# Attention heads on one Trainium2 core: each round's operations put in the order in which their inputs arrive

## The chip, the cores and the metric

One core of one Trainium2 chip runs the whole program in one launch. The metric is device time in microseconds (us). Engines: TensorE (PE in the rows, with PEld for its weight loads), VectorE (DVE), ScalarE (ACT), GpSimd (POOL) and SyncE (SP), which issues the DMA transfers.

## The reference, cut to what matters

Two layers over 512 frames of 1024 channels, float32. The first has a gated linear attention, the second chunked softmax attention with 16 heads of 64 channels; each is followed by a squared-ReLU MLP, and each sub-layer ends in a LayerNorm. The change sits in the softmax attention of the second layer:

```
q, k, v = jnp.split(u @ w_in + b_in, 3, axis=-1)
...
s = jnp.einsum('bhtd,bhjd->bhtj', qi, kb).astype(jnp.float32) + bias
p = jax.nn.softmax(jnp.where(mb, s, NEG_INF), axis=-1).astype(vb.dtype)
return jnp.einsum('bhtj,bhjd->bhtd', p, vb)
...
return o @ w_out
...
x = layer_norm(DEEPNORM_ALPHA * x + (1.0 + g1) * y, ln_g[i, 0], ln_b[i, 0])
```

## The kernel before

Activations lie with channels on partitions and the 512 frames along the row. A matrix product in float32 is made of three passes over a high and a low part of each operand, so for each weight tile and each activation ScalarE casts a high part and VectorE subtracts to get the low one.

Every engine runs its instructions strictly in the order in which the program text emits them: the wrapper `InOrder` (line 47 in every row is its line) chains each engine's instructions. So the text's order is each engine's queue, and an instruction that waits holds up all behind it on its engine. SyncE's DMA issues stand in text order too.

The attention (`att`) works on pairs of heads. `for p in range(-1, 6)` is the round: it makes q and k of head pair p+2 (`mtile`, 24 matmuls each, then `evac_qk`), works on the scores of heads 2p+2 (even) and 2p+3 (odd), and multiplies pair p with v. After the loop, heads 14 and 15 and the end of 12 and 13 are done in the functions `t1` to `t5`, which the list `ev` mixes with the output projection (`part`, called in `boundary`). The steps and how they look in the rows:

- `s_mm(h)`: TensorE, 8 matmuls, scores of one head (`ps<-ar,ar`).
- `s_a(h)`: VectorE adds the bias window (`af<-ps,ng,af`, 4 instructions) and takes maxima (3), with ScalarE copies; then GpSimd reduces the maximum over partitions (`mb<-af`, PARTITION_ALL_REDUCE).
- `s_b1(h)`: VectorE subtracts that maximum (`af<-af,mb`, 4). `s_b2(h)`: ScalarE's exponential (`af<-af` 128x1024 and 128x256). `s_b(h)` is both.
- `pv(h)`: TensorE, 4 matmuls with v (`ps<-af,vt`), which also give the softmax denominator.
- `fin1(p)`: the division's ScalarE part for a pair: two copies from PSUM (`af<-ps` 64x512), logarithm and exponential (`af<-af` 128x512). `fin2(p)`: its VectorE part (4 instructions: `af<-af` twice, `af<-ps,af` twice). `fin3(p)`: bias and split into high (ScalarE, `ar<-af,col`) and low (VectorE, `ar<-af,col,ar`).
- `q_hi`, `k_hi`: ScalarE casts of a new q or k (`ar<-f`), behind its evacuation (`f<-ps,bq` or `f<-ps,col`); `q_lo`, `k_lo`: VectorE's two subtractions (`ar<-f,ar` 64x512). The next pair's s_mm needs them.
- `s_pre(h)`: the DMA of a head's bias window (`af<-a_win`). `fill(n)`: weight transfers ahead of use.
- `ln_cols`: five VectorE operations on 8 columns that prepare a LayerNorm's scale and shift (`a`, `b`, `b`, `ag`, `ab`).

Before, fin1, fin2 and s_b1(odd) open a round, in this order, and s_b2(odd) comes after s_a(even); s_b2(even) closes it. The last round (p = 5) has an order of its own, in which s_b1(12) and s_b2(12) are left to `t1`. ln_cols for the following LayerNorm is called at the start of `boundary`, after the attention's loop is emitted.

Of the kernel before, what the change touches and what calls it, by code (L numbers as in the profile page):

```python
# [59 lines left out]
def trunk(ctx, tc, xT, c, ada, cols, gk1, gk2, w_qk, w_v, w_g, w_go, a_qk, a_v, a_tab,  # L60
# [239 lines left out]
    def mtile(u, f=True):  # L300
        w = next_w(f)
        ps = bank()
        for k in range(KT):
            mm3(ps, wk(w, k), uk(u, k), k == 0, k == KT - 1)
        return ps
# [665 lines left out]
    def att(u, es):  # L971
# [11 lines left out]
        def s_pre(h):  # L983
            sA, sB = act_f(), act_f()
            b = sB[:, 0, 256:S]
            nc.sync.dma_start(out=b, in_=a_win[h])
            sab[h] = sA, sB, b
# [4 lines left out]
        def s_mm(h):  # L992
            p = h // 2
            q, k = qs[p], ks[p]
            pss = [bank()[:, 0:S], bank()[:, 0:384]]
            pl = bank()
            pss += [pl[:, 0:256], pl[:, 256:S]]
            for j in range(4):
                ps = pss[j]
                n = max(W[j], 256)  # L1000
                js = slice(j * P, (j + 1) * P)
                T.matmul(ps[:, 0:n], k[:, h % 2, js], q[:, h % 2, S - n:S], start=True, stop=False)
                T.matmul(ps[:, 0:n], k[:, h % 2, js], ql[p][:, h % 2, S - n:S], start=False, stop=True)
            sps[h] = pss
# [26 lines left out]
        def s_b1(h):  # L1031
            s, sAf = st[h]
            mb = mbs[h]
            tt(V, s[0], s[0], mb, ALU.subtract)
            tt(V, s[1], s[1], mb[:, P:S], ALU.subtract)
            tt(V, s[2], s[2], mb[:, 256:S], ALU.subtract)
            tt(V, s[3], s[3], mb[:, 384:S], ALU.subtract)
# [15 lines left out]
        o = []  # L1053
# [3 lines left out]
        def fin1(p, pa, pb):  # L1057
            sy = act_f()
            s, y = sy[:, 0, :], sy[:, 1, :]
            A.copy(out=s[0:64, :], in_=pa[64:128, :])  # L1060
            A.copy(out=s[64:128, :], in_=pb[0:64, :])
            A.activation(out=y, in_=s, func=AF.Ln)
            A.activation(out=y, in_=y, func=AF.Exp, scale=-1.0)
            fin[p] = s, y, pa, pb

        def fin2(p):
            s, y, pa, pb = fin[p]
            tt(V, s, s, y, ALU.mult)
            stt(y, s, 2.0, y, ALU.subtract, ALU.mult)
            stt(s[0:64, :], pa[0:64, :], -1.0, y[0:64, :], ALU.mult, ALU.mult)  # L1070
            stt(s[64:128, :], pb[64:128, :], -1.0, y[64:128, :], ALU.mult, ALU.mult)
# [17 lines left out]
            fill(2)  # L1089
        prev = None  # L1090
        for p in range(-1, 6):
            pq = mtile(u, False)
            s_pre(2 * p + 2)
            s_pre(2 * p + 3)
            if prev:
                fin1(*prev)
                fin2(p - 1)
            if p >= 0:
                s_b1(2 * p + 1)
            s_mm(2 * p + 2)  # L1100
            q_hi, q_lo = evac_qk(p + 2, 0, pq)
            if p == 5:
                q_hi()
                q_lo()
                fill(2)
            if prev:
                fin3(p - 1)
            if p < 5:
                s_a(2 * p + 2)
                if p >= 0:  # L1110
                    s_b2(2 * p + 1)
                fill(2)
                q_hi()
                q_lo()
                pk = mtile(u, False)
                s_mm(2 * p + 3)
                k_hi, k_lo = evac_qk(p + 2, 1, pk)
                s_a(2 * p + 3)
                k_hi()
                s_b1(2 * p + 2)  # L1120
                k_lo()
                fill(2)
                s_b2(2 * p + 2)
            else:
                pk = mtile(u, False)
                k_hi, k_lo = evac_qk(p + 2, 1, pk)
                s_b2(2 * p + 1)
                k_hi()
                s_a(2 * p + 2)
                k_lo()  # L1130
                s_mm(2 * p + 3)
                s_a(2 * p + 3)
                fill(2)
            if p >= 0:
                prev = (p, pv(2 * p), pv(2 * p + 1))
        s_pre(14)
# [8 lines left out]

        def t1():
            s_mm(14)
            s_b1(12)
            s_a(14)
            s_b2(12)  # L1150
            fill(2)
            s_b(13)

        def t2():
            s_mm(15)
            s_a(15)
            fill(2)
            fin1(*prev)
            s_b(14)
            fin2(5)  # L1160

        def t3():
            s_b1(15)
            fin1(6, hold[12], hold[13])
            fin3(5)
            s_b2(15)
            fin2(6)
            fill(3)
# [65 lines left out]
    hs = run(u, 0)  # L1234
    u = boundary(hs, 0, G2, open_v, lambda: ln_cols(0, 1, (1, SH1, SC1)), None, vfill=vfill)
    cur["es"].close()
    o, ev, es = att(u, cur["es_v"])
    evac_h, run = mlp_fns()
    u = boundary(o, 1, G1, opener(es, 1), lambda: ln_cols(1, 0, (1, SH2, SC2)), evac_h, ev, late=True)
    hs = run(u, 1)  # L1240
    boundary(hs, 1, G2, same, lambda: ln_cols(1, 1, None), None, final=True)
    cur["es"].close()
# [52 lines left out]
```

## Time and profile before

| | |
|---|---|
| runs, median of 3 | 1212.07 us (1211.79 to 1212.17) |
| profiled execution | 1211.67 us, its span 1209.8 us |
| busy share of the span | TensorE 97%, VectorE 68%, ScalarE 46%, GpSimd 4% |
| granted TensorE clock, mean | 0.994 of full speed (2.4 GHz) |

The span is the time from the first to the last instruction that the profile holds; the rest of the execution lies around it. Times in the rows below are counted from the span's start. The attention's loop lies at about 637 to 767 us, its tail at 767 to 805. A row of a timeline gives start, duration, engine, line, operation, output and inputs, and the number of instructions merged in it; in brackets stands the idle time of the engine ahead of it and who ended it.

### The profile page before, as it was taken

Reading aid. Unit: us, or ns where it says so; the run is one execution under the profiler, and the core shown is the slowest. Engines: PE = TensorE matmul, PEld = TensorE weight load, DVE = VectorE, ACT = ScalarE, POOL = GpSimd, SP = SyncE. Lnnn points to the kernel's source line nnn. Section 1 sums busy time; section 2 is a strip of 40 time slices with the busy share of each in tenths; the row PEclk is TensorE's granted clock in tenths of the full one; section 3 lists DMA queues with packets and bytes.
Section 4 is the critical chain, followed back from the end, with each engine's and each line's share of the span. In section 5 each row is a group of like instructions: output and inputs, shape, how many; then the busy total and the mean of one; then the engine's idle time right before and its main releaser. Section 6 shows DMA issues by size and latency. Waiting matters only on the chain.

```text
span 1209.8 us, 15107 instructions
## 1 busy us (share of the span) xinstructions
PE 1177.0 (97%) x5742; PEld 981.0 (81%) x5742; DVE 827.5 (68%) x1359; ACT 555.0 (46%) x870; POOL 49.1 (4%) x61
## 2 busy tenths in 40 slices
PE   9999999999999999999999999998999999999995
PEld 5888888888888888888888777677988888888885
DVE  6788589877676676658835878988874443443467
ACT  4565555484243342343636656564742322422324
POOL 2000000000000000000011313200000000000000
PEclk9999999999999999999999999998999999999998
DMA  9756524028889889844125340330264232332302
GB/s 347 255 184 219 186 105 161 32 88 315 306 306 339 293 305 338 297 143 157 51 104 212 123 150 34 131 115 26 68 206 144 87 105 90 103 105 87 103 2 70
DMA packets 58283, 196.34 MB, mean 162 GB/s; under 512 B 6561, under 2 KB 10913, under 8 KB 58210
## 3 DMA queue, kind: packets, MB, share of 16 engines
q1 hardware_dynamic: 58210, 195.37, 46.7%
q8 instruction: 45, 0.74, 0.2%
q14 instruction: 28, 0.23, 0.1%
HBM read 174.37 MB, written 20.97 MB: 161 GB/s over the span
## 4 chain that ended last, share of the span: by engine, by line
PE 77%; DVE 15%; ACT 6%; issue 2%; DMA 0%; DVEq 0%; ACTq 0%
PE ps L47 76%; DVE af L47 6%; DVE x L47 4%; ACT af L47 3%; ACT ar L47 1%; DVE wlo L47 1%; DVE ar L47 1%; PE warm L47 1%; ACT u L47 1%; DVE d L47 1%; DVE flo L47 1%; DVE t L47 0%; DVE y L47 0%; DVE raw L47 0%; DMA raw<-f 0%
## 5 line engine op out<-in xcount | busy, mean ns | idle before, releaser
L47 PE MATMUL ps<-ar,whi 128*128 128x512 f32 (+1 forms) x2880 | 818.4, 372 | 0.2 <-DVE ar L47 0.2
L47 PEld LDWEIGHTS ps<-ar,whi 128*128 128x128 f32 x2880 | 524.4, 189 | 95.3 <-issue 2.4
L47 PE MATMUL ps<-ar,wlo 128*128 128x512 f32 (+1 forms) x1440 | 524.8, 371 | 0.1
L47 PEld LDWEIGHTS ps<-ar,wlo 128*128 128x128 f32 x1440 | 271.8, 189 | 47.0 <-DVE wlo L47 0.8
L47 ACT CAST whi<-raw 128x1024 fp32r<-128x1024 f32 (+1 forms) x169 | 169.6, 1012 | 202.5 <-PE ps L47 156.2
L47 DVE TENSOR_TENSOR wlo<-raw,whi 128x1024 fp32r<-128x1024 f32 x162 | 197.2, 1223 | 23.3 <-ACT whi L47 21.2
L47 DVE SCALAR_TENSOR_TENSOR x<-ps,mods,x 128x512 f32<-128x512 f32 (+1 forms) x96 | 63.2, 660 | 120.2 <-PE ps L47 119.8
L47 DVE TENSOR_TENSOR h<-r 128x512 f32<-128x512 f32 (+1 forms) x72 | 45.2, 633 | 79.1 <-ACT r L47 78.2
L47 ACT ACTIVATE r<-ps 128x512 f32<-128x512 f32 (+1 forms) x72 | 39.1, 548 | 126.5 <-PE ps L47 126.5
L47 DVE SCALAR_TENSOR_TENSOR raw<-raw,csil 128x1024 f32<-128x1024 f32 x80 | 96.8, 1218 | 0.0
L47 DVE TENSOR_TENSOR ar<-h,ar 128x512 fp32r<-128x512 f32 (+1 forms) x72 | 45.6, 633 | 39.6 <-ACT ar L47 38.5
L47 PE MATMUL ps<-ar,fhi 128*128 128x256 f32 (+1 forms) x320 | 69.0, 310 | 3.7 <-DVE ar L47 2.8
L47 ACT CAST ar<-h 128x512 fp32r<-128x512 f32 (+1 forms) x72 | 41.3, 573 | 50.4 <-DVE h L47 50.4
L47 PE MATMUL ps<-whi,ar 128*128 128x512 f32 x192 | 60.7, 390 | 0.0
L47 PEld LDWEIGHTS ps<-ar,fhi 128*128 128x128 f32 x320 | 52.0, 191 | 8.1 <-DVE ar L47 4.4
L47 PE MATMUL ps<-ar,flo 128*128 128x256 f32 (+1 forms) x160 | 48.8, 305 | 0.0
L47 ACT ACTIVATE af<-x 128x256 f32<-128x256 f32 (+1 forms) x48 | 23.0, 486 | 45.4 <-DVE x L47 42.2
L47 PEld LDWEIGHTS ps<-whi,ar 128*128 128x128 f32 x192 | 36.1, 188 | 7.6
L47 ACT ACTIVATE af<-af 128x1024 f32<-128x1024 f32 (+2 forms) x48 | 32.0, 698 | 20.9 <-DVE af L47 20.4
L47 ACT CAST fhi<-raw 128x1024 fp32r<-128x1024 f32 x30 | 31.2, 1050 | 21.6 <-DMA raw<-a_qk 13.0
L47 ACT ACTIVATE ar<-x,b,a 128x256 fp32r<-128x256 f32 x48 | 28.6, 595 | 25.8 <-DVE x L47 25.8
L47 PE MATMUL ps<-af,vt 128*128 128x512 f32 (+3 forms) x128 | 36.9, 436 | 2.0 <-ACT af L47 2.0
(141 smaller groups left out, 1024.8 us busy)
## 6 DMA issues: line engine op xcount, KB each, us to landing
raw<-f SPq DMA_DIRECT2D x128, 512.0 KB, 4.4
raw<-ada SPq DMA_DIRECT2D x80, 512.0 KB, 4.7
hraw<-ada SPq DMA_DIRECT2D x16, 512.0 KB, 9.0
raw<-a_qk SPq DMA_DIRECT2D x16, 512.0 KB, 5.6
khi_q<-fhi SPq DMA_DIRECT2D x14, 512.0 KB, 3.0
klo_q<-flo SPq DMA_DIRECT2D x14, 512.0 KB, 5.3
whi<-khi_q SPq DMA_DIRECT2D x14, 512.0 KB, 3.2
wlo<-klo_q SPq DMA_DIRECT2D x14, 512.0 KB, 4.4
```

The lines of the kernel that those rows point to most:

```text
L47: r = f(*a, **k)
```

## The change

Only the order of the text changes. In the rounds fin1 is followed by s_b1 and s_b2 of the odd head and only then by fin2; s_b1(even) goes ahead of s_a(odd); s_b2(even) becomes the last ScalarE work of the round. The last round is now like the others, so `t1` to `t3` lose head 12's part and take the rest in an order of the same kind. And ln_cols for the LayerNorm behind the attention is called ahead of the attention.

```
         for p in range(-1, 6):
+            h0 = 2 * p + 2
             pq = mtile(u, False)
-            s_pre(2 * p + 2)
-            s_pre(2 * p + 3)
+            s_pre(h0)
+            s_pre(h0 + 1)
             if prev:
                 fin1(*prev)
+            if p >= 0:
+                s_b1(h0 - 1)
+                s_b2(h0 - 1)
+            if prev:
                 fin2(p - 1)
-            if p >= 0:
-                s_b1(2 * p + 1)
-            s_mm(2 * p + 2)
+            s_mm(h0)
             q_hi, q_lo = evac_qk(p + 2, 0, pq)
-            if p == 5:
-                q_hi()
-                q_lo()
-                fill(2)
             if prev:
                 fin3(p - 1)
-            if p < 5:
-                s_a(2 * p + 2)
-                if p >= 0:
-                    s_b2(2 * p + 1)
-                fill(2)
-                q_hi()
-                q_lo()
-                pk = mtile(u, False)
-                s_mm(2 * p + 3)
-                k_hi, k_lo = evac_qk(p + 2, 1, pk)
-                s_a(2 * p + 3)
-                k_hi()
-                s_b1(2 * p + 2)
-                k_lo()
-                fill(2)
-                s_b2(2 * p + 2)
-            else:
-                pk = mtile(u, False)
-                k_hi, k_lo = evac_qk(p + 2, 1, pk)
-                s_b2(2 * p + 1)
-                k_hi()
-                s_a(2 * p + 2)
-                k_lo()
-                s_mm(2 * p + 3)
-                s_a(2 * p + 3)
-                fill(2)
+            s_a(h0)
+            q_hi()
+            q_lo()
+            fill(2)
+            pk = mtile(u, False)
+            s_mm(h0 + 1)
+            k_hi, k_lo = evac_qk(p + 2, 1, pk)
+            s_b1(h0)
+            s_a(h0 + 1)
+            k_hi()
+            k_lo()
+            s_b2(h0)
+            fill(2)
...
         def t1():
             s_mm(14)
-            s_b1(12)
+            s_b1(13)
+            fin1(*prev)
             s_a(14)
-            s_b2(12)
+            s_b2(13)
+            fin2(5)
             fill(2)
-            s_b(13)
 
         def t2():
             s_mm(15)
             s_a(15)
+            fin3(5)
+            s_b1(14)
+            s_b2(14)
             fill(2)
-            fin1(*prev)
-            s_b(14)
-            fin2(5)
 
         def t3():
             s_b1(15)
             fin1(6, hold[12], hold[13])
-            fin3(5)
             s_b2(15)
             fin2(6)
...
+    lnc1 = ln_cols(1, 0, (1, SH2, SC2))
     o, ev, es = att(u, cur["es_v"])
     evac_h, run = mlp_fns()
-    u = boundary(o, 1, G1, opener(es, 1), lambda: ln_cols(1, 0, (1, SH2, SC2)), evac_h, ev, late=True)
+    u = boundary(o, 1, G1, opener(es, 1), lambda: lnc1, evac_h, ev, late=True)
```

VectorE's queue from the end of one round into the next, before (the last s_b1 instruction of head 6, k_lo, fin2(1), s_b1(7), fin3(1), the first of s_a(8); tiles carry their program numbers, mb982 is head 6's maximum and mb991 head 7's):

```order
L47 TENSOR_TENSOR af970_5806<-af970_5806,mb982_5855 128x128
L47 TENSOR_TENSOR ar990_5907<-f989_5905,ar990_5907 64x512 x2
L47 TENSOR_TENSOR af1001_5975<-af1001_5975 128x512
L47 SCALAR_TENSOR_TENSOR af1001_5975<-af1001_5975 128x512
L47 SCALAR_TENSOR_TENSOR af1001_5975<-ps994_5934,af1001_5975 64x512
L47 SCALAR_TENSOR_TENSOR af1001_5975<-ps995_5939,af1001_5975 64x512
L47 TENSOR_TENSOR af972_5809<-af972_5809,mb991_5918 128x512
L47 TENSOR_TENSOR af972_5809<-af972_5809,mb991_5918 128x384
L47 TENSOR_TENSOR af973_5810<-af973_5810,mb991_5918 128x256
L47 TENSOR_TENSOR af972_5809<-af972_5809,mb991_5918 128x128
L47 SCALAR_TENSOR_TENSOR ar1008_6005<-af1001_5975,col_75,ar1008_6005 128x512
L47 SCALAR_TENSOR_TENSOR af997_5969<-ps1002_5988,ng_5404,af998_5970 128x256
```

The same place in after (the last instruction of s_a(7), k_lo, s_b1(7), fin2(1), fin3(1), the first of s_a(8)):

```order
L47 TENSOR_TENSOR af977_5819<-af977_5819,af976_5818 128x128
L47 TENSOR_TENSOR ar994_5916<-f993_5914,ar994_5916 64x512 x2
L47 TENSOR_TENSOR af976_5818<-af976_5818,mb995_5931 128x512
L47 TENSOR_TENSOR af976_5818<-af976_5818,mb995_5931 128x384
L47 TENSOR_TENSOR af977_5819<-af977_5819,mb995_5931 128x256
L47 TENSOR_TENSOR af976_5818<-af976_5818,mb995_5931 128x128
L47 TENSOR_TENSOR af1005_5984<-af1005_5984 128x512
L47 SCALAR_TENSOR_TENSOR af1005_5984<-af1005_5984 128x512
L47 SCALAR_TENSOR_TENSOR af1005_5984<-ps998_5943,af1005_5984 64x512
L47 SCALAR_TENSOR_TENSOR af1005_5984<-ps999_5948,af1005_5984 64x512
L47 SCALAR_TENSOR_TENSOR ar1012_6016<-af1005_5984,col_75,ar1012_6016 128x512
L47 SCALAR_TENSOR_TENSOR af1001_5978<-ps1006_5999,ng_5413,af1002_5979 128x256
```

Head 6's subtractions are gone from here (they now stand ahead of s_a(7)), and head 7's moved from behind fin2 to ahead of it, directly behind k_lo; fin3 now follows fin2 directly.

ScalarE's queue across the border of two rounds, before (exponentials of head 8, fin1(3), evacuation of q, fin3(3), the copies of s_a(10), exponentials of head 9):

```order
L47 ACTIVATE af1024_6132<-af1024_6132 128x1024
L47 ACTIVATE af1025_6133<-af1025_6133 128x256
L47 COPY af1055_6301<-ps1048_6260 64x512
L47 COPY af1055_6301<-ps1049_6265 64x512
L47 ACTIVATE af1055_6301<-af1055_6301 128x512 x2
L47 ACTIVATE f1059_6325<-ps1050_6270,bq8_103 128x512
L47 ACTIVATE ar1062_6331<-af1055_6301,col_75 128x512
L47 COPY af1051_6295<-ps1056_6314 128x256
L47 COPY af1051_6295<-ps1057_6315 128x128
L47 COPY af1052_6296<-af1051_6295 128x128
L47 ACTIVATE af1026_6135<-af1026_6135 128x1024
L47 ACTIVATE af1027_6136<-af1027_6136 128x256
```

In after (k_hi, exponentials of head 8, fin1(3), exponentials of head 9, evacuation of q, fin3(3)):

```order
L47 CAST ar1048_6242<-f1047_6240 64x512 x2
L47 ACTIVATE af1028_6141<-af1028_6141 128x1024
L47 ACTIVATE af1029_6142<-af1029_6142 128x256
L47 COPY af1059_6310<-ps1052_6269 64x512
L47 COPY af1059_6310<-ps1053_6274 64x512
L47 ACTIVATE af1059_6310<-af1059_6310 128x512 x2
L47 ACTIVATE af1030_6144<-af1030_6144 128x1024
L47 ACTIVATE af1031_6145<-af1031_6145 128x256
L47 ACTIVATE f1063_6336<-ps1054_6279,bq8_103 128x512
L47 ACTIVATE ar1066_6342<-af1059_6310,col_75 128x512
```

The odd head's exponentials moved from behind the copies of the next s_a to directly behind fin1, ahead of the evacuation of q. The even head's keep their place on ScalarE behind k_hi, but what they wait for (s_b1 of that head) now stands a whole s_a earlier on VectorE.

In the tail, VectorE's queue in before (s_b1(14), fin2(5), s_b1(15)):

```order
L47 TENSOR_TENSOR af1104_6590<-af1104_6590,mb1117_6632 128x512
L47 TENSOR_TENSOR af1104_6590<-af1104_6590,mb1117_6632 128x384
L47 TENSOR_TENSOR af1105_6591<-af1105_6591,mb1117_6632 128x256
L47 TENSOR_TENSOR af1104_6590<-af1104_6590,mb1117_6632 128x128
L47 TENSOR_TENSOR af1125_6685<-af1125_6685 128x512
L47 SCALAR_TENSOR_TENSOR af1125_6685<-af1125_6685 128x512
L47 SCALAR_TENSOR_TENSOR af1125_6685<-ps1102_6580,af1125_6685 64x512
L47 SCALAR_TENSOR_TENSOR af1125_6685<-ps1103_6585,af1125_6685 64x512
L47 TENSOR_TENSOR af1106_6593<-af1106_6593,mb1122_6679 128x512
L47 TENSOR_TENSOR af1106_6593<-af1106_6593,mb1122_6679 128x384
L47 TENSOR_TENSOR af1107_6594<-af1107_6594,mb1122_6679 128x256
L47 TENSOR_TENSOR af1106_6593<-af1106_6593,mb1122_6679 128x128
```

In after the same fin2(5) stands two heads' work earlier (the last of s_a(14), fin2(5), s_a(15)):

```order
L47 TENSOR_TENSOR af1109_6606<-af1109_6606,af1108_6605 128x128
L47 TENSOR_TENSOR af1117_6628<-af1117_6628 128x512
L47 SCALAR_TENSOR_TENSOR af1117_6628<-af1117_6628 128x512
L47 SCALAR_TENSOR_TENSOR af1117_6628<-ps1106_6595,af1117_6628 64x512
L47 SCALAR_TENSOR_TENSOR af1117_6628<-ps1107_6600,af1117_6628 64x512
L47 SCALAR_TENSOR_TENSOR af1110_6608<-ps1120_6667,ng_5413,af1111_6609 128x256
L47 SCALAR_TENSOR_TENSOR af1110_6608<-ps1121_6668,ng_5413,af1111_6609 128x256
L47 SCALAR_TENSOR_TENSOR af1111_6609<-ps1122_6669,ng_5413,af1111_6609 128x256
L47 SCALAR_TENSOR_TENSOR af1110_6608<-ps1122_6669,ng_5413,af1111_6609 128x128
L47 TENSOR_TENSOR af1111_6609<-af1110_6608 128x384
L47 TENSOR_TENSOR af1111_6609<-af1111_6609 128x256
L47 TENSOR_TENSOR af1111_6609<-af1111_6609,af1110_6608 128x128
```

It moved ahead of s_a(15), so the reduction that s_a(14) starts runs beside it.

## Rows read from the trace of the kernel before

**Rows 1.** Page, busy time of the engines: us, share of the span, instructions.

```profile
PE 1177.0 (97%) x5742; PEld 981.0 (81%) x5742; DVE 827.5 (68%) x1359; ACT 555.0 (46%) x870; POOL 49.1 (4%) x61
```

**Rows 2.** Timeline of TensorE: s_mm(4), s_mm(6), s_mm(12), first use of fin3(7).

```profile
679.40 1.44 PE L47 MATMUL ps<-ar,ar 128*128 128x512 f32 x8
...
697.21 1.45 PE L47 MATMUL ps<-ar,ar 128*128 128x512 f32 x8
...
754.52 1.57 PE L47 MATMUL ps<-ar,ar 128*128 128x512 f32 x8 [1.02 <-DVE ar L47]
...
804.87 0.50 PE L47 MATMUL ps<-ar,fhi 128*128 128x512 f32 x1 [1.59 <-DVE ar L47]
```

**Rows 3.** Timeline of VectorE: fin2(1), s_b1(7), fin3(1), s_a(8)..., fin2(4).

```profile
698.12 0.69 DVE L47 TENSOR_TENSOR af<-af 128x512 f32<-128x512 f32 x1 [2.54 <-ACT af L47]
...
701.09 1.70 DVE L47 TENSOR_TENSOR af<-af,mb 128x512 f32<-128x512 f32 x4
702.71 0.74 DVE L47 SCALAR_TENSOR_TENSOR ar<-af,col,ar 128x512 fp32r<-128x512 f32 x1
703.48 1.53 DVE L47 SCALAR_TENSOR_TENSOR af<-ps,ng,af 128x256 f32<-128x256 f32 x4
...
708.79 1.53 DVE L47 SCALAR_TENSOR_TENSOR af<-ps,ng,af 128x256 f32<-128x256 f32 x4
...
711.48 2.54 DVE L47 TENSOR_TENSOR af<-af,mb 128x512 f32<-128x512 f32 x4
...
757.73 0.69 DVE L47 TENSOR_TENSOR af<-af 128x512 f32<-128x512 f32 x1 [2.54 <-ACT af L47]
```

**Rows 4.** Timeline of ScalarE: k_hi, exponentials of head 6, fin1 of the pair before.

```profile
710.06 1.26 ACT L47 CAST ar<-f 64x512 fp32r<-64x512 f32 x2
714.05 1.37 ACT L47 ACTIVATE af<-af 128x1024 f32<-128x1024 f32 x2 [2.73 <-DVE af L47]
715.44 1.19 ACT L47 COPY af<-ps 64x512 f32<-64x512 f32 x2
716.66 1.30 ACT L47 ACTIVATE af<-af 128x512 f32<-128x512 f32 x2
```

**Rows 5.** Timeline of VectorE: first instructions of s_a(5), s_a(13) and fin2(7).

```profile
688.91 1.53 DVE L47 SCALAR_TENSOR_TENSOR af<-ps,ng,af 128x256 f32<-128x256 f32 x4
...
769.50 1.52 DVE L47 SCALAR_TENSOR_TENSOR af<-ps,ng,af 128x256 f32<-128x256 f32 x4
...
797.69 0.69 DVE L47 TENSOR_TENSOR af<-af 128x512 f32<-128x512 f32 x1 [1.48 <-ACT af L47]
```

**Rows 6.** Timeline of VectorE in the last round: s_a(12) and k_lo behind it.

```profile
764.53 1.53 DVE L47 SCALAR_TENSOR_TENSOR af<-ps,ng,af 128x256 f32<-128x256 f32 x4
...
767.34 2.13 DVE L47 TENSOR_TENSOR ar<-f,ar 64x512 fp32r<-64x512 f32 x2
```

**Rows 7.** Timeline of GpSimd: reductions of heads 7 and 12.

```profile
711.73 2.08 POOL L47 PARTITION_ALL_REDUCE mb<-af  x1 [3.49 <-DVE af L47]
...
767.50 2.17 POOL L47 PARTITION_ALL_REDUCE mb<-af  x1 [12.80 <-DVE af L47]
```

**Rows 8.** Timeline of ScalarE: evacuation of q in round 1; fin3(7)'s ScalarE part.

```profile
679.60 0.69 ACT L47 ACTIVATE f<-ps,bq 128x512 f32<-128x512 f32 x1 [1.39 <-PE ps L47]
...
800.66 0.73 ACT L47 ACTIVATE ar<-af,col 128x512 fp32r<-128x512 f32 x1 [0.16 <-DVE af L47]
```

**Rows 9.** Timeline of VectorE: ahead of the attention's first q; ln_cols and what follows.

```profile
638.65 0.68 DVE L47 TENSOR_TENSOR ar<-f,ar 64x512 fp32r<-64x512 f32 x1 [9.34 <-ACT ar L47]
...
772.20 0.16 DVE L47 TENSOR_TENSOR a<-col,mods 128x8 f32<-128x8 f32 x1
...
773.58 1.68 DVE L47 TENSOR_TENSOR af<-af,mb 128x512 f32<-128x512 f32 x4
```

**Rows 10.** DMA issues, 630 to 835 us: size of one, median us from issue to landing.

```profile
af<-a_win SPq DMA_DIRECT2D x16, 128.0 KB, 3.8
```

**Rows 11.** The tile mb: GpSimd's 16 reductions, ns min/median/max, first and last start.

```profile
L47 POOL PARTITION_ALL_REDUCE mb<-af x16: 1784/2053/2168, 651.7 to 783.9; - x16
```

## The prediction

> **What bounds the kernel now.** I read the page's engine shares first, then TensorE's timeline over the attention, then VectorE's, then ScalarE's, each time asking who waits. TensorE is busy 97% of the span [rows 1], so an order of work can win only where TensorE stands still, and the timeline says where. A round of the attention loop is 17.81 us of TensorE's own work: s_mm(4) starts at 679.40 and s_mm(6) at 697.21, and TensorE waits for nothing between. The three rounds from s_mm(6) to s_mm(12) take 57.31, which is 3.88 more than three of 17.81, and s_mm(12) had to wait 1.02 for VectorE's k_lo [rows 2]. VectorE shows that this is its own pace: fin2 starts at 698.12 and, three rounds on, at 757.73, which is 19.87 a round, already in the rounds in which TensorE does not wait yet. And at the head of each stands the same hole, 2.54 us idle until ScalarE [rows 3]. ScalarE's rows say why: the even head's exponential (1.37) starts only when VectorE's s_b1 is done, at 714.05, and the division's copies (1.19), logarithm and exponential (1.30) stand behind it, to 717.96 [rows 4]. VectorE's fin2 at 717.99 waits for all of that. So the round is VectorE's queue: 19.87 with 2.54 of waiting in it.
>
> Behind the loop comes the tail. s_a(13) starts at 769.50 and fin2(7) at 797.69, 28.19 later [rows 5]; behind it comes fin3(7), for which TensorE waits 1.59 [rows 2]. From fin2(7) on both programs are the same on all engines, so the change is worth what fin2(7) moves.
>
> **The change part by part.** No instruction is added or removed; the instructions only exchange places on their engines.
>
> *The round.* VectorE's new order is s_a(even), q_lo, s_b1(even), s_a(odd), k_lo, s_b1(odd), fin2, fin3. s_b1 now stands one pair of subtractions (q_lo or k_lo) behind the s_a whose maximum GpSimd reduces for it, where before there was more between, so the reduction decides. The last round of before has this sequence once: s_a(12) at 764.53, k_lo at 767.34, the reduction from 767.50 for 2.17, so to 769.67 [rows 6, 7]. That is 5.14 after s_a's start; I take 5.15 for s_b1, 0.2 later than VectorE would be there by itself (767.34 + 2.13 = 769.47). s_b1 takes 1.62 where no reduction runs (701.09 to 702.71). fin2 takes 2.97 (698.12 to 701.09). fin3's subtraction 0.77 (702.71 to 703.48) [rows 3]. Ahead of it comes a new wait: fin3's ScalarE part needs fin2's end and takes 0.73 [rows 8], and VectorE has nothing between the two; before, s_b1(odd) stood there. With the two handovers I take 0.80. What is queued behind it is s_a(even), whose scores are ready. Sum: 2 x (5.15 + 1.62) + 2.97 + 0.80 + 0.77 = 18.1 for a round, against 19.87. The 2.54 is gone because ScalarE now reaches fin1 while VectorE is still in k_lo, the wait and s_b1(odd): counted from s_a(odd) (708.79 in [rows 3]), k_hi ends at 2.5 (711.32 in [rows 4]), the even exponential at 3.9, fin1 at 6.4, and s_b1(odd) at 6.8; pv, which TensorE does right behind s_mm(odd), is there by then. From below the round is bounded by TensorE's 17.81; from above I take 18.9, if each half loses 0.4 more.
>
> *Where it starts.* The first rounds follow TensorE in both kernels. In round 1 of after, fin3's ScalarE part stands behind the evacuation of q, which cannot start before TensorE has finished the tile, 679.60 as now, and takes 0.69 [rows 8]. So s_a(4) starts at 679.60 + 0.69 + 0.73 + 0.05 + 0.77 = 681.85 and s_a(5) 6.8 later, at 688.6; before it is 688.9 [rows 5]. Four rounds on is s_a(13): 688.6 + 4 x 18.1 = 761.0, against 769.50. That is 8.5 gained.
>
> *Is TensorE fed?* Then s_mm(10) comes at 679.40 + 3 x 17.81 = 732.8 and s_mm(12) at 750.6. Each needs the first of k_lo's two subtractions, done 3.4 after the s_a(odd) before it starts (2.69 and 0.7). s_a(9) is at 688.6 + 2 x 18.1 = 724.8 and s_a(11) at 742.9, so k_lo is there at 728.2 and 746.3, more than 4 ahead. TensorE does not wait inside the loop. s_mm(14) has no q tile ahead of it and waits for k_lo until 764.4 (768.17 before, by the end of k_lo's first half in [rows 6]); but the tail is VectorE's.
>
> *The tail.* From s_a(13) in after, in us: s_b1(13) ends at 6.8, s_a(14) at 9.5 (2.69, from 708.79 to 711.48), fin2(5) at 13.1, s_a(15) at 15.8, fin3(5) at 16.6, s_b1(14) at 19.1, s_b1(15) at 20.7. In fin2(5) and s_b1(14) a reduction runs beside: 0.7 and 0.9 more, as 2.54 against 1.70 for the same four subtractions [rows 3]. Then ScalarE is late: the exponential of 14 (1.37) ends at 20.5 and fin1(6) (2.49) at 23.0, so VectorE waits 2.3; fin2(6) ends at 26.0. fin3(6)'s ScalarE part ends at 26.7, and fin1(7) at 29.2. fin2(7) starts there: 29.2 instead of 28.19, so 1.0 is given back. Without the two collisions it would be 27.6; with 0.9 more at each of two further places 31.
>
> *The column work.* ln_cols' five small operations fill 772.20 to 773.58, part of the 28.19 that is not in the 29.2. They move to a place where VectorE sits idle for 9.34 [rows 9]; without that cover they would cost the same 1.4 there.
>
> *Transfers.* SP's order is the same. Of what it waits for, the bias window a_win comes closest: it lands 3.8 after its issue [rows 10], and that of head 12 is issued when s_mm(11) is done, a mtile and more ahead of s_mm(12) at 750.6, for an s_a(12) near 754 (761.0 - 6.8). Hidden.
>
> *A rule against it.* The row: while the reduction of 711.73 ran (2.08), the four subtractions took 0.84 longer; and beside that of 767.50 the pair k_lo ended before 769.50, ahead of the reduction's end [rows 5 to 7]. The Trainium skill, SBUF — State Buffer, Who interferes with whom, says that a Vector instruction with two SBUF inputs and a GpSimd one that reads SBUF exclude each other for the whole instruction. The trace agrees that they collide and differs on how long. By the rule k_lo would end after the reduction and the round would be 19.5, an estimate with its result under C; by the row it is 18.1.
>
> Sum: 8.5 - 1.0 = 7.5 gained. The profiled execution took 1211.67, of which 1209.80 is the span; it would be 1204.2. The median of the runs shown is 0.4 above it, so 1204.6.
>
> **The rivals.** A: TensorE becomes the bound. If the reductions end in 1.78, as the shortest of the 16 does [rows 11], nothing waits for them, the rounds are 17.81, s_a(13) comes at 759.8 and the tail is 27.6: fin2(7) at 787.4, 10.3 gained, 1201.8. Against it: where k_lo followed its s_a at once, as all pairs do now, the reduction took 2.17.
>
> B: the tail and the rounds give back more. Tail 31 and rounds of 18.4: 688.6 + 73.6 + 31 = 793.2, 4.5 gained, 1207.6. For it: in the tail the exponentials of 14 and 15 and fin1(6) stand in one ScalarE queue, and pv(14) and pv(15) wait for them.
>
> C: the change doesn't do what it says, since q_lo and k_lo are held to the end of the reduction. Then s_b1 starts 0.7 later in each half, 1.4 a round: 19.5, s_a(13) at about 767.3, 2.2 ahead; fin2(5) and s_b1(14), held as long, make the tail 30.5, so the 2.2 is given back: 1212.
>
> D: slower. s_b1 is exposed to the reduction twice a round. The round is 17.7 + 2w, with w the wait at each s_b1, 0.2 in my sum; at w = 1.1 it is 19.87 and nothing is won. At w = 1.5 it is 20.7: s_a(13) at 771.4 instead of 769.50, and with the tail's 1.0 the time is 1215.0. For it: no row of before shows VectorE waiting for GpSimd, so the handover is unmeasured. Against it: 2.17 is the longest reduction of the 16 [rows 11], so w = 1.1 would need a handover of 0.9, where the one from VectorE to ScalarE takes 0.03 (714.02 to 714.05 in [rows 3, 4]).
>
> **How the numbers follow.** The forecast (5.5 to 9 gained) gets 0.62, A 0.12, B 0.13, C 0.07, D 0.06. The range reaches from A to a little beyond B, 1201.6 to 1208.6: forecast, A and B hold 0.87, less a little at the edges. About 0.2%, 2.4 us, is what a measurement of this kernel tells from no change. Forecast, A and B are faster by more: 0.87; C is the same: 0.07; D slower: 0.06.
>
> **What would show it.** Right: VectorE's 2.54 before fin2 gone in all rounds; a new wait of some 0.8 of fin3's subtraction for ScalarE, and short waits (0.2 to 0.3) of s_b1 for GpSimd; s_mm(12) without a wait, near 750.6; s_a(13) near 761, fin2(7) near 790. Wrong: s_b1's waits over 1 us (D), q_lo and k_lo over 2.8 (C), fin2(7) more than 31 behind s_a(13) (B), rounds of 17.8 with VectorE idle (A). A longer wait of fin2 for fin1, or of s_mm for a PSUM bank that fin2 frees late, would be something that I have not seen.

## The result, and the profile after

The changed kernel takes 1203.70 us (median of 5 runs, 1203.25 to 1204.67) where the kernel before, run beside it, takes 1212.01: a ratio of 0.9932, interval 0.9920 to 0.9943. That is 8.3 us, and 7.5 were forecast; the forecast time was 1204.6.

TensorE's busy share rose a point, with the same 5742 matmuls. The page's line on the engines:

```profile
PE 1175.6 (98%) x5742; PEld 981.6 (82%) x5742; DVE 825.9 (69%) x1359; ACT 555.4 (46%) x870; POOL 51.5 (4%) x61
```

TensorE's timeline of after: s_mm(6), s_mm(12), s_mm(14), the first use of fin3(7), and the first product of the LayerNorm's sums behind the attention.

```profile
696.92 1.45 PE L47 MATMUL ps<-ar,ar 128*128 128x512 f32 x8
...
750.35 1.45 PE L47 MATMUL ps<-ar,ar 128*128 128x512 f32 x8
...
763.71 1.54 PE L47 MATMUL ps<-ar,ar 128*128 128x512 f32 x8 [0.86 <-DVE ar L47]
...
796.57 0.50 PE L47 MATMUL ps<-ar,fhi 128*128 128x512 f32 x1 [1.03 <-DVE ar L47]
...
820.10 2.08 PE L47 MATMUL ps<-af,ones_c 128*128 128x256 f32 x4 [5.48 <-DVE af L47]
```

Inside the loop no row has a bracket any more: the three rounds from s_mm(6) to s_mm(12) take 53.43, three times 17.81, where they took 57.31 [rows 2]. What is left are short waits behind the loop, and the one of 5.48 at the LayerNorm, which was there before. That product in the kernel before:

```profile
828.46 2.08 PE L47 MATMUL ps<-af,ones_c 128*128 128x256 f32 x4 [5.54 <-DVE af L47]
```

VectorE in after, one round (from s_a(8), at the top, to s_a(10), at the bottom), then s_a(13) and the tail's marks:

```profile
699.44 1.53 DVE L47 SCALAR_TENSOR_TENSOR af<-ps,ng,af 128x256 f32<-128x256 f32 x4
...
702.13 2.12 DVE L47 TENSOR_TENSOR ar<-f,ar 64x512 fp32r<-64x512 f32 x2
704.49 1.70 DVE L47 TENSOR_TENSOR af<-af,mb 128x512 f32<-128x512 f32 x4 [0.23 <-POOL mb L47]
706.11 1.52 DVE L47 SCALAR_TENSOR_TENSOR af<-ps,ng,af 128x256 f32<-128x256 f32 x4
...
708.91 2.13 DVE L47 TENSOR_TENSOR ar<-f,ar 64x512 fp32r<-64x512 f32 x2
711.27 1.70 DVE L47 TENSOR_TENSOR af<-af,mb 128x512 f32<-128x512 f32 x4 [0.23 <-POOL mb L47]
712.89 0.68 DVE L47 TENSOR_TENSOR af<-af 128x512 f32<-128x512 f32 x1
...
716.66 0.75 DVE L47 SCALAR_TENSOR_TENSOR ar<-af,col,ar 128x512 fp32r<-128x512 f32 x1 [0.84 <-ACT ar L47]
717.44 1.53 DVE L47 SCALAR_TENSOR_TENSOR af<-ps,ng,af 128x256 f32<-128x256 f32 x4
...
760.07 1.52 DVE L47 SCALAR_TENSOR_TENSOR af<-ps,ng,af 128x256 f32<-128x256 f32 x4
...
769.54 0.68 DVE L47 TENSOR_TENSOR af<-af 128x512 f32<-128x512 f32 x1
770.26 1.41 DVE L47 SCALAR_TENSOR_TENSOR af<-af 128x512 f32<-128x512 f32 x1
...
776.50 4.14 DVE L47 TENSOR_TENSOR af<-af,mb 128x512 f32<-128x512 f32 x8
783.06 0.69 DVE L47 TENSOR_TENSOR af<-af 128x512 f32<-128x512 f32 x1 [2.42 <-ACT af L47]
...
789.39 0.69 DVE L47 TENSOR_TENSOR af<-af 128x512 f32<-128x512 f32 x1 [1.47 <-ACT af L47]
```

The hole of 2.54 at the head of fin2 [rows 3] is gone: fin2 starts at 712.89 with no bracket. In its place stand the waits that were forecast, 0.23 for GpSimd ahead of each s_b1 and 0.84 for ScalarE ahead of fin3. From s_a(8) to s_a(10) it is 18.00; s_a(4) starts at 681.43 and s_a(12) at 753.40, so the mean of four rounds is 17.99 instead of 19.87. ScalarE shows why: k_hi, the even exponentials, fin1 and the odd exponentials of the same round.

```profile
707.37 1.26 ACT L47 CAST ar<-f 64x512 fp32r<-64x512 f32 x2
708.65 1.36 ACT L47 ACTIVATE af<-af 128x1024 f32<-128x1024 f32 x2
710.04 1.19 ACT L47 COPY af<-ps 64x512 f32<-64x512 f32 x2
711.26 1.30 ACT L47 ACTIVATE af<-af 128x512 f32<-128x512 f32 x2
713.00 1.37 ACT L47 ACTIVATE af<-af 128x1024 f32<-128x1024 f32 x2 [0.45 <-DVE af L47]
```

The even exponentials follow k_hi without a wait, where they waited 2.73 for s_b1 [rows 4]; fin1 ends 6.4 behind the start of s_a(odd), before VectorE is through s_b1(odd).

The gain adds up along VectorE: s_a(13) moved from 769.50 [rows 5] to 760.07, which is 9.43; from there to fin2(7) it is 29.32 instead of 28.19, so 1.13 is given back; fin2(7) is 8.30 earlier, and TensorE's first product of the sums 8.36 (828.46 before, 820.10 now). The two spans differ by only 7.3, because the profiled execution of after lost about 1 us more in the clock behind the 5.48. The same 10 us from that product on in both kernels (before, then after; the columns are busy time of PE, PEld, DVE, ACT and POOL, granted clock, DMA share, GB/s):

```profile
828.46:838.46 10.00, 10.00 (x65) 9.64 (x66) 7.72 (x21) 4.42 (x11) 0.00 (x0) 0.81 0.00 0
```

```profile
820.10:830.10 10.00, 10.00 (x57) 9.64 (x58) 7.73 (x21) 4.42 (x10) 0.00 (x0) 0.70 0.00 0
```

0.11 of 10 us is 1.1 us of TensorE's full-speed work lost, because it stayed longer at the lower of its two levels (1.2 GHz) after a wait of the same length. It is not the change's: in the 14 profiled executions of before, after and the runs below this mean lies between 0.70 and 0.85; the first run below, with the new order in its rounds and 5.54 of waiting there, has 0.81, and the kernel before with nothing but ln_cols moved has 0.70 (from 827.94 on). So the experiments are read by two marks as well as by their times: s_a(13), the loop's end, and that first product of the sums, called the mark below (before 828.46, after 820.10). A mark shifts from execution to execution too: in after and the four runs below with the same loop, s_mm(4) comes between 679.12 (after) and 679.61, and in before at 679.40. So 0.28 of the 8.36 is there already at s_mm(4), ahead of what the new order gains, and a mark by itself is good to about 0.5.

### The profile page after: what moved, and what is told of

The parts are those of the page before. It is cut to its first block, busy times and chain, and to the rows that moved or that the text cites. A ratio compares the mean times of both kernels' runs of the same rounds, so it can differ in the third digit from the quotient of the medians.

```text
span 1202.5 us, 15104 instructions
## 1 busy us (share of the span) xinstructions
PE 1175.6 (98%) x5742; PEld 981.6 (82%) x5742; DVE 825.9 (69%) x1359; ACT 555.4 (46%) x870; POOL 51.5 (4%) x61
## 4 chain that ended last, share of the span: by engine, by line
PE 77%; DVE 14%; ACT 4%; issue 2%; POOL 1%; DMA 1%; SPq 0%; DVEq 0%; ACTq 0%; POOLq 0%
PE ps L47 77%; DVE af L47 6%; DVE x L47 4%; ACT af L47 2%; DVE wlo L47 1%; ACT ar L47 1%; POOL mb L47 1%; DVE flo L47 1%; DMA hraw<-ada 1%; ACT u L47 0%; DVE d L47 0%; DVE t L47 0%; DVE ar L47 0%; DVE y L47 0%; DVE raw L47 0%
## 5 line engine op out<-in xcount | busy, mean ns | idle before, releaser
L47 DVE TENSOR_TENSOR ar<-f,ar 64x512 fp32r<-64x512 f32 x32 | 32.2, 1005 | 12.8 <-ACT ar L47 12.2
L47 POOL PARTITION_ALL_REDUCE mb<-af x16 | 33.8, 2112 | 121.2 <-DVE af L47 121.2
```

Of the source, the lines that this page charges most:

```text
L47: r = f(*a, **k)
```

## Experiments

Each was timed in five rounds beside the kernel before.

**The loop's order alone.** The rounds p = -1 to 4 as in the changed kernel, all else as before.

```
for p in range(-1, 6):
    if p < 5: <round of after>
    else:     <last round of before>
...           <t1 to t3, ln_cols of before>
```

> Only the rounds p = -1 to 4 have the new order; the last round, t1 to t3 and the place of ln_cols are those of before. Theory (VectorE's queue in the rounds is the whole gain, the new last round and tail give nothing): s_a(11) at 742.1 as in the changed kernel, s_a(13) near 760.8 behind the old last round, fin2(7) 28.2 behind it as in before, so near 789.0, and the time 1203.3 (1202.5 to 1204.5), no worse than the changed kernel's 1203.7. Rival (the last round with the order of the others and the new tail carry a share, since the last round of before took 21.0 from s_a(11) to s_a(13) and now takes 18.0): 3 us are missing, 1206.5 or more.

Measured: 1207.24, ratio 0.9960 (0.9947 to 0.9972); mark 823.74. s_a(11) comes at 742.37, about as in after (742.06), but s_a(13) at 764.79, and by the mark 3.6 of the gain are missing (by the time 3.5). VectorE's and ScalarE's rows of this kernel, from s_a(12) on, and from k's evacuation on:

```profile
755.71 1.52 DVE L47 SCALAR_TENSOR_TENSOR af<-ps,ng,af 128x256 f32<-128x256 f32 x4
761.25 1.01 DVE L47 TENSOR_TENSOR af<-af 128x384 f32<-128x384 f32 x2 [4.02 <-ACT af L47]
...
764.79 1.53 DVE L47 SCALAR_TENSOR_TENSOR af<-ps,ng,af 128x256 f32<-128x256 f32 x4
```

```profile
757.58 0.69 ACT L47 ACTIVATE f<-ps,col 128x512 f32<-128x512 f32 x1 [2.69 <-PE ps L47]
758.17 1.35 ACT L47 ACTIVATE af<-af 128x1024 f32<-128x1024 f32 x2
759.42 1.23 ACT L47 CAST ar<-f 64x512 fp32r<-64x512 f32 x2
760.68 0.54 ACT L47 COPY af<-ps 128x256 f32<-128x256 f32 x2
```

s_a(12) starts at 755.71 and stands still 4.02 in its middle: its maxima need ScalarE's copy of the scores (760.68), and in the last round's old order that copy stands behind k's evacuation, for which ScalarE waits until TensorE has finished the tile (757.58), the odd exponentials and k_hi. In the kernel before VectorE came to s_a(12) only at 764.53 [rows 6]; k_hi ended there at 764.93 and the copy ran at 765.05, in time for the maxima, so nothing showed. The theory that the rounds are the whole gain fell; the last round's new order is what lets the gain of the loop through.

**The last round and the tail alone.** The reverse: rounds -1 to 4 and ln_cols of before, last round and t1 to t3 of after.

```
for p in range(-1, 6):
    if p == 5: <round of after>
    else:      <round of before>
...            <t1 to t3 of after>
```

> Only the last round and t1 to t3 have the new order; the rounds p = -1 to 4 and ln_cols' place are those of before. Theory: fin2(4) still stands at 757.7 behind ScalarE's late exponential, s_a(13) comes at 769.1, the new tail takes 29.3, fin2(7) at 798.4: 1212.7 (1212.0 to 1213.5), no gain. Rival (the last round and the tail carry a share): 3 us faster, 1209.

Measured: 1213.04, ratio 1.0009 (1.0000 to 1.0017); s_a(13) at 768.80, mark 829.29. As the theory had it: the new last round and tail alone win nothing. s_a(13) comes 0.70 earlier, but fin2(7) stands 29.78 behind it (798.58) instead of 28.19. Together with the first run: 4.7 for the loop alone, -1.1 for the rest with the columns left where they were, 8.3 for all. The parts don't add; the last round is worth much only when the loop arrives early: behind the old rounds it brings s_a(13) forward by 0.70, behind the new ones by 4.72 (764.79 to 760.07).

**ln_cols' place, in both kernels.** First before with ln_cols moved, then after with it moved back.

```
+    lnc1 = ln_cols(1, 0, (1, SH2, SC2))          (before: moved; after: taken back)
     o, ev, es = att(u, cur["es_v"])
```

> The kernel before with ln_cols called ahead of the attention, nothing else. Theory: the five operations stood in the tail's 28.19 on VectorE's path, and in their new place VectorE idles, so 1.0 to 1.4 are gained: 1210.8 (1210.5 to 1211.2). Rival (TensorE's or ScalarE's waits in the tail take it back): 1212.0, no change.

Measured: 1211.73, ratio 0.9998 (0.9989 to 1.0007); fin2(7) at 797.17, only 0.52 earlier.

> The changed kernel with ln_cols called behind the attention's loop again, as in before. Theory: its five operations (1.38) stand ahead of s_b1(13) in the tail; they cover the 0.23 for which that waits on the reduction, so the tail grows by 1.15, fin2(7) near 790.5 instead of 789.39, 1204.8 (1204.2 to 1205.4). In the kernel before the same move moved fin2(7) by only 0.52, since s_b1(12) then fell beside a reduction. Rival (the tail's waits for ScalarE, 2.42 and 1.47, take it up): 1203.7.

Measured: 1203.97, ratio 0.9931 (0.9919 to 0.9944); fin2(7) 29.61 behind s_a(13) instead of 29.32, mark 820.48. Neither time can be told from that of the kernel without the edit. Both theories asked too much. VectorE in before-with-ln_cols-moved (s_b1(12)), then in after-with-ln_cols-back (the first of its five operations, s_b1(13)):

```profile
772.22 2.53 DVE L47 TENSOR_TENSOR af<-af,mb 128x512 f32<-128x512 f32 x4
```

```profile
765.11 0.17 DVE L47 TENSOR_TENSOR a<-col,mods 128x8 f32<-128x8 f32 x1
...
765.62 1.69 DVE L47 TENSOR_TENSOR af<-af,mb 128x512 f32<-128x512 f32 x4
```

In after the five operations take 0.51 (765.11 to 765.62) and cover the 0.23 for which s_b1(13) waits without them, which leaves 0.28. In before they took 1.38 [rows 9], because the reduction of head 13 started among them (772.45); take them away, and the reduction's toll falls on s_b1(12), 2.53 here instead of 1.68. So 0.51 was theirs and 0.87 the reduction's, which stays wherever VectorE's work goes.

**Half the round undone.** In the first of two kernels the odd head's half stands as before, in the second the even head's.

```
 first:                          second:
-    s_b1(h0 - 1)               -    s_b1(h0)
-    s_b2(h0 - 1)                    s_a(h0 + 1)
     fin2(p - 1)                     k_hi()
+    s_b1(h0 - 1)               +    s_b1(h0)
...                                  k_lo()
     s_a(h0)                         s_b2(h0)
+    s_b2(h0 - 1)
```

> The changed kernel, but in the rounds the odd head's half stands as in before (fin1, fin2, s_b1(odd), the odd exponentials behind s_a(even)); s_b1(even) stays ahead of s_a(odd). Theory (fin2 waits for fin1, which ends 6.4 behind the start of s_a(odd), whatever VectorE does; s_b1(odd) fills that wait): VectorE waits 1.5 ahead of fin2, fin3's wait of 0.85 and the odd s_b1's of 0.23 are gone, the round is 18.5 instead of 17.99, s_a(13) 2.0 to 2.5 later, 1206.0 (1205.3 to 1206.7). Rival (s_b1(even) alone frees ScalarE, the rest of the new order is worth nothing): rounds of 18.0, 1203.7.

Measured: 1207.67, ratio 0.9963 (0.9951 to 0.9976); rounds of 18.74, s_a(13) at 763.35, mark 823.38.

> The changed kernel, but in every round s_b1(even) stands behind s_a(odd) and k_hi again, as in before; the odd head's half stays as changed. Theory: the even exponential ends 6.6 behind the start of s_a(odd) and fin1 9.1, VectorE has work until 8.3 and waits 0.8 ahead of fin2, the round is 18.6 instead of 17.99, s_a(13) comes near 762.6; k_lo of the last round, now behind s_b1(12), holds TensorE at s_mm(14) for 4 to 5 us instead of 0.86, as in the run with the odd half undone: 1207.9 (1206.8 to 1209.0). Rival (the odd half alone hides the late exponential): rounds of 18.0, 1203.7 to 1204.5.

Measured: 1209.10, ratio 0.9974 (0.9964 to 0.9984); rounds of 18.6, s_a(13) at 762.53, mark 825.09. VectorE's fin2 in the first and the second kernel, then TensorE's s_mm(14) in each:

```profile
713.59 0.69 DVE L47 TENSOR_TENSOR af<-af 128x512 f32<-128x512 f32 x1 [1.55 <-ACT af L47]
...
732.32 0.69 DVE L47 TENSOR_TENSOR af<-af 128x512 f32<-128x512 f32 x1 [1.55 <-ACT af L47]
```

```profile
734.55 0.69 DVE L47 TENSOR_TENSOR af<-af 128x512 f32<-128x512 f32 x1 [0.81 <-ACT af L47]
```

```profile
766.98 2.33 PE L47 MATMUL ps<-ar,ar 128*128 128x512 f32 x8 [4.11 <-DVE ar L47]
```

```profile
768.62 2.69 PE L47 MATMUL ps<-ar,ar 128*128 128x512 f32 x8 [5.71 <-DVE ar L47]
```

The waits ahead of fin2 are 1.55 and 0.81, as worked out from fin1's end (1.5 and 0.8). So either half alone leaves a part of the hole, and only both close it. Both times lie above the range that was expected (to 1206.7 and to 1209.0). In the first the round is 0.24 longer than expected; q_hi now stands behind the odd exponentials and q_lo waits 0.40 for it, in place of the 0.23 ahead of s_b1(even). By fin2(7) the first is 3.27 later than after (792.66), as its loop ends 3.28 later. The second is 4.97 later (794.36): 2.46 from the loop, 1.53 from s_b1(12), which with this order stands behind s_a(13), and 0.98 more of waiting ahead of fin2(7) (2.45 instead of 1.47), for TensorE stood 5.71 at s_mm(14) and pv(15) and fin1(7) come late. The expectation priced behind the loop only the wait at s_mm(14), at 4 to 5; it was longer, and what it cost fin2(7) is the smaller part.

**The reductions taken out.** s_b1 subtracts a tile of zeros, so the softmax is computed without its maximum.

```
+        ng0 = ac.tile([P, S], F32, name="mb0")
+        G.memset(ng0, 0.0)
...
-            mb = ab_.tile([P, S], F32, tag="mb", name=nm("mb"))
-            G.partition_all_reduce(mb, mx, P, bass_isa.ReduceOp.max)
+            mb = ng0
```

> The changed kernel without GpSimd's maximum over partitions: s_b1 subtracts a tile of zeros that is set once; everything else stays. Theory (the reduction costs a round 0.46 of waits and 1.4 of slower pairs, and the tail 1.5 in fin2(5) and s_b1(14)): VectorE's work in a round falls to 16.8 with a short wait for fin1, TensorE's 17.81 becomes the round, s_a(13) near 758.6, the tail some 2.4 shorter, all of TensorE's waits in the tail (0.86, 0.46, 1.03) mostly gone: 1201.3 (1200.8 to 1202.5), and k_lo takes 1.4 instead of 2.13. Rival (the pairs are slow for another reason than the reduction): k_lo stays at 2.1 and the round at 17.5 or more, s_a(13) near 759.5, the tail stays at 29: 1203.

Measured: 1200.59, ratio 0.9905 (0.9891 to 0.9918); s_a(13) at 758.74, mark 817.38. The pairs q_lo and k_lo in the rounds, in after and then in this kernel (ns of one subtraction, shortest, median, longest; first and last start):

```profile
L47 DVE TENSOR_TENSOR ar<-f,ar x18: 674/1050/1441, 684.1 to 756.8; 64x512 fp32r<-64x512 f32 x18
```

```profile
L47 DVE TENSOR_TENSOR ar<-f,ar x18: 674/686/691, 684.5 to 756.4; 64x512 fp32r<-64x512 f32 x18
```

With no reduction beside them all 18 take 0.69; with it half of them take 1.4. VectorE's rounds are TensorE's 17.81, and TensorE has no wait from the loop to the mark. That is rival A's bound, and it lies 3.1 below the changed kernel.

**fin3 behind s_a(even).** The new wait of 0.84 is covered.

```
-            if prev:
-                fin3(p - 1)
             s_a(h0)
+            if prev:
+                fin3(p - 1)
```

> The changed kernel, but in every round s_a(even) goes ahead of fin3, so that VectorE has work while ScalarE does fin3's part. Theory (the wait of 0.85 is a real price of the new order and VectorE still sets the round): VectorE's round falls to 16.9, so TensorE's 17.81 becomes the round, s_a(13) comes at 758.6, the tail stays 29.3, fin2(7) near 788.0, 1202.3 (1201.7 to 1203.0). Rival (the round is TensorE's already, s_a(13) cannot move): 1203.7.

Measured: 1202.76, ratio 0.9923 (0.9910 to 0.9937); s_a(13) at 758.65, fin2(7) at 787.97, mark 818.69. VectorE's s_a(8) and s_a(10) in this kernel:

```profile
715.74 1.57 DVE L47 SCALAR_TENSOR_TENSOR af<-ps,ng,af 128x256 f32<-128x256 f32 x4 [0.80 <-PE ps L47]
...
733.54 1.57 DVE L47 SCALAR_TENSOR_TENSOR af<-ps,ng,af 128x256 f32<-128x256 f32 x4 [0.83 <-PE ps L47]
```

Each now waits for the scores, the releaser is PE, and the rounds are 17.81 (s_a(12) comes at 751.35): with 0.85 less, VectorE is no longer the bound of the loop. s_a(13) is 1.4 earlier than in after: half of that is there at s_a(5) already (687.38, after 688.10), the rest is four rounds of 0.18 less. The time alone does not settle it, since the interval of its ratio overlaps that of after (0.9920 to 0.9943).

**The old tail.** After, with t1 to t3 as before, less head 12's part.

```
 def t1(): s_mm(14); s_a(14); fill(2); s_b(13)
 def t2(): s_mm(15); s_a(15); fill(2); fin1(*prev); s_b(14); fin2(5)
 def t3(): s_b1(15); fin1(6, ...); fin3(5); s_b2(15); fin2(6); fill(3)
```

> The changed kernel with t1 to t3 in the order of before, less head 12's part, which the last round does now. Theory (the new tail gives back 1.0, because fin2(6) waits 2.4 behind the exponentials of head 14): VectorE is through its queue earlier, fin2(7) waits only for pv(15) and fin1(7), near 788.3 instead of 789.39, 1202.7 (1201.9 to 1203.5). Rival (the old tail brings back TensorE's waits of 1.2 for a free PSUM bank and 0.7 for the exponentials): 1203.7 to 1205.

Measured: 1202.40, ratio 0.9921 (0.9907 to 0.9934); mark 818.84. fin2(7) comes 27.49 behind s_a(13) (760.59 to 788.08) instead of 29.32. TensorE's first use of fin3(7), for which it waits 0.15 where it waited 1.03:

```profile
795.25 0.50 PE L47 MATMUL ps<-ar,fhi 128*128 128x512 f32 x1 [0.15 <-DVE ar L47]
```

So the new order of the tail costs 1.8 on VectorE and, with this last round, 1.3 of the time by the medians; here too the intervals of the ratios overlap, but the runs do not (1202.05 to 1202.91, after 1203.25 to 1204.67). The forecast's 1.0 was counted against the tail of before, which had head 12's s_b1 and ln_cols besides.

**Two single waits of the tail.** In one kernel fin1(6) goes ahead of the exponentials of head 14, in the other fin3(7) ahead of the weights' split.

```
 t2: -  s_b2(14)                        t5:    fin2(7)
 t3:    fin1(6, hold[12], hold[13])         +  fin3(7)
     +  s_b2(14)                               fill(5)
        s_b2(15)                            -  fin3(7)
```

> The changed kernel, but in the tail fin1(6) goes ahead of the exponentials of head 14 on ScalarE, so that fin2(6) need not wait for both. Theory (the 2.42 ahead of fin2(6) is not what holds fin2(7); that is the way over the exponential of 14, pv(14), pv(15) and fin1(7)): fin2(6) starts at 780.7 instead of 783.06, but pv(14) waits 1.7 instead of 0.46, pv(15) and fin1(7) come later, fin2(7) near 789.9: 1204.2 (1203.5 to 1204.9). Rival (VectorE's largest wait in the tail is its price): fin2(7) 1.5 to 2.4 earlier, 1202.3 or less.

Measured: 1203.35, ratio 0.9925 (0.9911 to 0.9939); mark 819.69.

> The changed kernel, but at the tail's end fin3(7) goes ahead of the weights' split (three VectorE operations of 1.17 each) that stood between it and fin2(7). Theory (the tail ends where TensorE waits for fin3(7), 1.03, and behind it VectorE sets the pace): TensorE's 1.03 is gone, VectorE reaches the residual's updates about when it does now but waits 0.8 less behind them: 1202.8 (1202.3 to 1203.4). Rival (VectorE only gets the same work later, nothing gained): 1203.7.

Measured: 1203.64, ratio 0.9928 (0.9916 to 0.9941); mark 820.24. VectorE's fin2(6) and fin2(7) in the first, and TensorE's last wait ahead of the mark in the second:

```profile
780.95 0.68 DVE L47 TENSOR_TENSOR af<-af 128x512 f32<-128x512 f32 x1
...
788.96 0.69 DVE L47 TENSOR_TENSOR af<-af 128x512 f32<-128x512 f32 x1 [3.17 <-ACT af L47]
```

```profile
798.56 1.12 PE L47 MATMUL ps<-x,ones_h 128*128 128x512 f32 x2 [1.03 <-DVE x L47]
```

In the first the 2.42 ahead of fin2(6) is gone, and 1.70 of it comes back ahead of fin2(7), which waits 3.17 instead of 1.47; counted from s_a(13) the tail is 0.8 shorter (28.51), not longer by 0.5 as the theory said, since pv(14) waited 0.88 and not 1.7. The time can't be told from that of after. In the second TensorE's 1.03 at fin3(7) is gone and stands, as 1.03, at the next thing that VectorE hands it: the theory fell, VectorE's queue is the bound there.

**Both edits that won.** fin3 behind s_a(even), and the old tail.

> Two edits together on the changed kernel: fin3 behind s_a(even) in the rounds, and t1 to t3 in the order of before without head 12's part. Theory: s_a(13) at 758.65, s_mm(14) and fin3(7) without a wait, so TensorE is the bound through loop and tail as in the run without reductions: 1201.3 (1200.6 to 1202.0). Rival (both edits shorten the same path and only one counts): 1202.4.

Measured: 1201.13 (1200.64 to 1201.16), ratio 0.9907 (0.9894 to 0.9921). TensorE has no wait from the loop up to the mark:

```profile
817.31 2.08 PE L47 MATMUL ps<-af,ones_c 128*128 128x256 f32 x4 [5.53 <-DVE af L47]
```

This beats the changed kernel by 2.6, and the runs of the two do not overlap; its mark (817.31) stands with that of the kernel without reductions (817.38): loop and tail are TensorE's now.

## Why the prediction was right

**The round.** 19.87 was taken to be VectorE's queue with 2.54 of waiting for a late ScalarE, and 18.1 was forecast; it is 17.99, made of the terms that were named: the wait at s_b1 0.23 (0.2 taken), the wait at fin3 0.84 (0.80), the slowed pair 2.13. That the hole came of the late even exponentials, with nothing left on VectorE to fill it, is shown by undoing either half: with the exponentials early but s_b1(odd) behind fin2 it is 1.55, with s_b1(odd) ahead of fin2 but the exponentials late 0.81, in each case where fin1's end puts it. Neither alone is the whole cause. That it is VectorE's queue that sets the round, and not TensorE, is shown by fin3 moved: 0.85 less on VectorE, and the round falls to TensorE's 17.81.

**Start and loop's end.** s_a(5) came at 688.10 (688.6 forecast), s_a(13) at 760.07 (761.0): 0.5 from the start and 0.4 from the round. Of the 0.5, 0.28 is luck: TensorE finished q's tile that much earlier than in before (679.32), which is within the shift from one execution to another, and in the other runs with this loop s_a(13) comes between 760.15 and 760.59. s_mm(12) is at 750.35 with no wait (750.6), s_mm(14) at 763.71 (764.4) with 0.86, all 0.3 to 0.9 early.

**The tail.** 29.32, with 29.2 forecast. fin2(6) waits 2.42 (2.3), the two collisions are there: in fin2(5) one operation takes 1.41 instead of 0.69 (770.26), and s_b1 of heads 14 and 15 together 4.14. Against the tail of before 1.13 is given back (1.0 forecast). That was the price against a tail with more work in it: with the last round changed, the old order takes 27.49, which the forecast did not weigh.

**What the forecast did not have.** It took the gain to be the rounds', and the last round as one more of them. The first experiment shows that it is the gate: with its old order s_a(13) comes 4.72 later and, as the old tail is shorter, 3.5 of the gain stay behind, in a queue on ScalarE that the trace of before could not show as a wait. And ln_cols' 1.38, said to be part of the old tail, was 0.51 of work and 0.87 of the reduction. Neither changed the sum, since both stood in the change and the tail was added up from its pieces.

**The rivals.** A (TensorE becomes the bound, 1201.8) is what the two edits of the last run reach, 1201.13, but not by A's condition: the reductions take 2.02 to 2.20 there. In the changed kernel they take 2.01 to 2.19, not 1.78, and VectorE stays 0.18 a round behind. B: neither tail nor rounds gave back more. C: k_lo is through at 693.03 in the round where the reduction runs from 691.04 for 2.19, so it is not held to its end. D: the wait at s_b1 is 0.23, far from 1.1.

## What to carry to other kernels

An idle time at the same place of every round, ended by an engine that is itself waiting, is a matter of order: write down, from one start, when each engine's result is there, and emit in that order; then add the waits that the new order makes. A piece of the program that shows no wait can hold back a gain that comes from ahead of it: look what its queue waits for once the work arrives earlier. And taking away the longest wait of a stretch is worth nothing where another way to its end is as long: 2.42 taken away made the tail 0.8 shorter, with nothing that the time shows, and 1.03 gave nothing.

## What the runs showed of the hardware

A reduction over partitions on GpSimd slows one VectorE operation, not all that run beside it. The two subtractions of k_lo, from a round of after, and the reduction:

```profile
690.90 0.69 DVE L47 TENSOR_TENSOR ar<-f,ar 64x512 fp32r<-64x512 f32 x1
```

```profile
691.62 1.41 DVE L47 TENSOR_TENSOR ar<-f,ar 64x512 fp32r<-64x512 f32 x1
```

```profile
691.04 2.19 POOL L47 PARTITION_ALL_REDUCE mb<-af  x1 [4.59 <-DVE af L47]
```

The one that had begun is not slowed; the next takes 1.41 instead of 0.69 and ends at 693.03, 0.2 before the reduction. The reduction waits as well: it takes 2.01 to 2.20 where such a VectorE operation is running when it starts, and 1.78 or 1.79 where none is, as ahead of q_lo in before, whose first subtraction is slowed all the same:

```profile
686.58 1.78 POOL L47 PARTITION_ALL_REDUCE mb<-af  x1 [11.37 <-DVE af L47]
```

```profile
686.78 1.38 DVE L47 TENSOR_TENSOR ar<-f,ar 64x512 fp32r<-64x512 f32 x1 [0.40 <-ACT ar L47]
```

The toll is the same 0.7 to 0.9 wherever it falls: on the second subtraction of s_b1 in before (0.84 for the four, [rows 3]), on fin2's second operation (770.26), on ln_cols. The Trainium skill, SBUF — State Buffer, Who interferes with whom, has it that whichever of the two engines is first holds the port pair that they share for its whole instruction; the traces agree that one waits for the other and that a single VectorE operation is not disturbed once it runs, and differ on the length. An operation of 0.69 that ends 1.99 behind the reduction's start was let in at 1.3 of its 2.19; the running subtraction had ended at 0.55, so VectorE was held off for some 0.75. In the rows of before, by the same count, it was let in at 0.9 of 1.78. These are estimates from the rows shown, and the spans that the profile gives for GpSimd are rough. Without reductions all of it is gone, 0.69 for each of 18. The price of a reduction to VectorE is thus a fixed toll in every order of work that was run here. Whether it goes where VectorE has nothing with two SBUF inputs to do just then, no run tried.

A long wait of TensorE costs more than itself. Behind the 5.71 at s_mm(14) in the kernel with the even half undone, the eight products take 2.69 at a granted clock of 0.50 (1.2 GHz), and over the 10 us from 768 on it is 0.76:

```profile
768.00:778.00 10.00, 9.38 (x37) 8.05 (x38) 9.73 (x20) 5.82 (x12) 2.05 (x1) 0.76 0.04 14
```

Behind the 0.86 of after they take 1.54 at 1.00 (2.4 GHz).
